# A decoder trunk on one core: the blocks of x's features spaced 136 words apart instead of 128, hi and lo parts shifted against each other

## Chip, cores, metric

One core of one Trainium2 chip runs the kernel. The metric is the device time of one execution in microseconds. Before the change three runs took 2485.54, 2493.08 and 2496.03 us; their median, 2493.08 us, is the time to compare with.

## What is computed

The input x is 256 tokens by 2048 features, float32. Two layers follow: a gated DeltaNet layer with its MLP, then a shared K/V projection, a differential-attention layer and its MLP. Nearly all of the arithmetic is in the products of 256 rows of activations with large weight matrices:

```
def gated_deltanet(x, w_in, conv_w, a_log, dt_bias, norm_w, w_out):
    p = x @ w_in                                 # 2048 -> 8192 + 32
    qkv = causal_conv_silu(p[..., :GDN_CONV_CH], conv_w)
    ...                                          # beta, g from the last 32 columns; delta rule
    return o.reshape(B, S, GDN_V_WIDTH) @ w_out  # 2048 -> 2048

def sq_relu_mlp(x, w_up, w_down):                # 2048 -> 8192 -> 2048
    return jnp.square(jax.nn.relu(x @ w_up)) @ w_down

def reference(x, ...):
    for l in range(DEPTH):                       # DEPTH = 2
        h = gated_deltanet(...) if l < N_A_LAYERS else diff_attention(..., k_sh, v_sh, ...)
        x = layer_norm(ALPHA * x + h, ln_g[l, 0], ln_b[l, 0])
        x = layer_norm(ALPHA * x + sq_relu_mlp(x, w_up[l], w_down[l]), ln_g[l, 1], ln_b[l, 1])
        if l == N_A_LAYERS - 1:
            k_sh, v_sh = shared_kv(x, shared_w_kv)   # 2048 -> 4096
    return x
```

## The kernel before

Every large product runs with the activations as the stationary operand of TensorE (loaded by LDWEIGHTS, 128 features by 128 tokens) and the weights streaming past as the moving operand, 512 columns at a time. To keep float32 accuracy both are split into a high and a low part of type float32r, and three matmuls, hi*hi, hi*lo and lo*hi, are accumulated (lines 174, 175, 176 in `product`). Each of the three has a LDWEIGHTS of its own.

`run` walks over the products: for each step of usually four k-tiles it takes token tile 0, then token tile 1; within a token tile the k-tiles in turn, within a k-tile the two column groups g of 512 columns. A k-tile thus gives six matmuls in a row, 174, 175, 176 for g = 0 and again for g = 1. Between the steps `pump` puts smaller pieces of work (convolution, scores, transposes) on TensorE.

The activations of a product come from one of two places:

- `xhl`, one constant tile, holds the features of the residual stream: for each part (hi, lo), token tile t and k-tile k a block of 128 tokens on 128 partitions. It is the stationary operand of x @ w_in, of both MLPs' w_up, of w_kv and of w_q: 30 products of 192 matmuls. `load_x` fills it first, `ln_apply` after each layer norm, both through `to_features` (four transposes by TensorE, then `split`: hi by ScalarE on line 78, lo by VectorE on line 79).
- blocks `blk` of 8 KB hold everything else: the squared ReLU for w_down, the outputs of both mixers for w_out and w_o. These are 20 products of 192 matmuls.

The moving operand is always a tile `wh` or `wl`, which `load_weights` makes from a DMA'd tile `wr` (ScalarE line 78, VectorE or GpSimd line 79). `gates` is the one place where x's features are the moving operand: on lines 424 and 425 the 32 columns of beta and alpha (in a `blk`) are stationary, and per k-tile one matmul streams hi and lo together (512 columns) and one streams hi alone (256 columns).

Where the tiles lie matters here. In the built program `xhl` begins at byte 17024 of each partition, which is 128 past a multiple of 512. Its blocks are 512 bytes apart, its token tiles 8 KB, its parts 16 KB, so that every block begins 128 past a multiple of 512. The pools `raw`, `hi`, `lo`, `blk` and `sm` follow the constants; the first `wh` begins at byte 69952, the first `wl` at 94528, the first `blk` at 119104, the first `sm` at 209216, each 320 past a multiple of 512, and all of their buffers and column groups are multiples of 512 further.

```
        self.sm_pool = pool("sm", 8)
        ...
        self.xhl = self.const.tile([P, 2, NT, KD, P], F32R, name="xhl")
    ...
    def x_stat(self, k, part, t):
        return self.xhl[:, part, t, k]
```

Of the kernel before, what the change touches and what calls it, by code (L numbers as in the profile page):

```python
# [27 lines left out]
SC = 4  # L28
ALPHA = 4.0**0.25
# [6 lines left out]
class Trunk:  # L36
    """Products run with the activations as the stationary operand and the weights streaming past them.

    Both operands are split exactly into two parts of 12 significant bits (float32r); three passes,
    hi*hi + hi*lo + lo*hi, give a float32 product. Activations for a product are kept with the features  # L40
    on the partitions, [128, (hi, lo), token tile, k-tile, token]; everything else is [token, feature].
    """

    def __init__(self, ctx, tc):
        self.tc, self.nc = tc, tc.nc
        pool = lambda name, bufs, **kw: ctx.enter_context(tc.tile_pool(name=name, bufs=bufs, **kw))
        nc = self.nc
        self.const = pool("const", 1)
        self.raw = pool("raw", 4)
        self.hi = pool("hi", 6)  # L50
        self.lo = pool("lo", 6)
        self.blk_pool = pool("blk", 11)
        self.sm_pool = pool("sm", 8)
        self.tiny = pool("tiny", 3)
        self.dram = pool("dram", 2, space=bass.MemoryType.DRAM)
        self.acc = pool("acc", 4, space=PSUM)
        self.ps_pool = pool("ps", 4, space=PSUM)
        self.plan, self.units, self.chain, self.pending, self.last = [], deque(), deque(), deque(), None
        self.ident = self.const.tile([P, P], F32, name="ident")
        make_identity(nc, self.ident)  # L60
        self.xhl = self.const.tile([P, 2, NT, KD, P], F32R, name="xhl")
        self.mask = self.const.tile([P, T], F32, name="mask")
        self.head_w = self.const.tile([P, P], F32, name="head_w")
# [17 lines left out]
    def rsqrt(self, dst, x, shape):  # L81
        """dst = x ** -0.5 for x > 0 (float32 accuracy: a guess from the exponent and three Newton steps)."""
        v = self.nc.vector
        y, t = self.small(shape, "rsq_y"), self.small(shape, "rsq_t")
        v.tensor_scalar(y.bitcast(I32), x.bitcast(I32), -0.5, float(0x5F3759DF), op0=ALU.mult, op1=ALU.add)
        for i in range(3):
            v.tensor_tensor(t, y, y, op=ALU.mult)
            v.scalar_tensor_tensor(t, t, -0.5, x, op0=ALU.mult, op1=ALU.mult)
            v.scalar_tensor_tensor(dst if i == 2 else y, t, 1.5, y, op0=ALU.add, op1=ALU.mult)

    def rsqrt_column(self, dst, x):
        """rsqrt of a column [128, 1] in fewer steps: (y y x - 3) y, Newton's step less its factor -1/2.

        The guess is scaled by a with -8192 a^27 = 1, which the three factors left out multiply back to 1.
        """
        v = self.nc.vector
        y, t = self.small([1], "rsq_y1"), self.small([1], "rsq_t1")
        a = -(8192.0 ** (-1.0 / 27.0))
        guess = RSQRT_GUESS - 2.0**31
        v.tensor_scalar(y.bitcast(I32), x.bitcast(I32), -0.5, guess, op0=ALU.mult, op1=ALU.add)  # L100
        for i, c in enumerate((3 * a**2, 12 * a**6, 768 * a**18)):
            v.scalar_tensor_tensor(t, y, x, y, op0=ALU.mult, op1=ALU.mult)
            last = v.scalar_tensor_tensor(dst if i == 2 else y, t, c, y, op0=ALU.subtract, op1=ALU.mult)
        return last

    def after(self, ins):
        """What is traced inside takes its turn on the engine of ins behind it."""
        return self.tc.issue_after(ins.ins) if ins is not None else nullcontext()

    def x_stat(self, k, part, t):  # L110
        return self.xhl[:, part, t, k]

    @staticmethod
    def act_stat(act):
        return lambda k, part, t: Trunk.act_view(act[k // 4])[:, part, t, k % 4]

    def gemm(self, nk, wsrc, stat, evac, pre=None, rate=1, need=None, cuts=None):
        """Plans a product: evac(g, t, psum) gets out[token tile t, columns g * 512 ..] of the 1024 columns of wsrc(k)."""
        self.plan.append((nk, wsrc, stat, evac, pre, rate, need, cuts or [SC] * (nk // SC)))

    def run(self):
# [4 lines left out]
        for j, (i, s, n) in enumerate(steps):  # L126
# [8 lines left out]
            for t in range(NT):  # L135
                # at the end of the second token tile one bank is done before the other, and evacuated meanwhile
# [41 lines left out]
    def later(self, fn, *args):  # L178
        """Work on the side of the products: emitted between them, a unit at a time."""
        self.units.append((fn, args))  # L180

    def soon(self, fn, *args):
        """A step of an evac that the tensor engine takes a few products later, when its operand is ready."""
        self.pending.append((fn, args))

    def pump(self, n):
        """Emits n units, and one of the slow chain, whose steps wait for transfers."""
# [12 lines left out]
    def transpose4(self, src):  # L200
        """[128, 512] -> PSUM [128, 4, 128], each 128 x 128 block transposed."""
# [5 lines left out]
    def to_features(self, src, dst, t):  # L207
        """src [128 tokens, 512] -> dst [128 features, (hi, lo), token tile, 4, 128 tokens] at token tile t."""
        self.split(dst[:, 0, t], dst[:, 1, t], self.transpose4(src))

    @staticmethod
    def act_view(a):
        return a.rearrange("p (s t k q) -> p s t k q", s=2, t=NT, k=4)
# [12 lines left out]
    def load_x(self, x):  # L226
        """The features of x by quarters: the first at once, the others between the first products."""
# [3 lines left out]
        def turn(t, q):  # L231
            with self.after(self.last):
                self.to_features(r[t][:, cut(q)], self.xhl[:, :, :, q * 4 : q * 4 + 4], t)
# [27 lines left out]
    def ln_apply(self, ln, t, q):  # L261
# [5 lines left out]
        if ln["out"] is None:  # L267
            self.to_features(xc, self.xhl[:, :, :, q * 4 : q * 4 + 4], t)
# [3 lines left out]
    def ln_finish(self, ln, t, own):  # L272
        """The last normalisation of a token tile: chunks below own on DVE, the others on ACT and Pool beside it."""
# [13 lines left out]
    def residual(self, n, alpha, ln=None):  # L287
        """The evac that adds a product's columns n * 1024 .. to the residual, and normalises it after the last."""
# [26 lines left out]
    def ends(n):  # L315
        """Before a normalisation the first token tile ends early, so that its rows are ready when the second ends."""
        return [5, 5, 6] if n == D // C - 1 else None

    def project_out(self, w, act, g, b, pre=None, need=None, out=None):
        """residual <- LayerNorm(alpha * residual + act @ w)."""  # L320
# [44 lines left out]
    def gated_deltanet(self, x, w_in, conv_w, a_log, dt_bias, norm_w, w_out, g, b, out=None):  # L365
        """The delta rule over all 256 tokens at once, two blocks of 128.

        With k2 = 2 k etc. (silu(y) = (tanh(y / 2) + 1) y / 2), S = |k2|^2 + 4 eps and c = beta / S:
        M = I + strict((k2 k2^T) c_j decay_ij), M y = v sqrt(S) / 2, o = 2 |q2|^-1 dk^-1/2 tril((q2 k2^T) c_j decay_ij) y.
        Matrices are kept transposed, [j, i]; the inverses of M's diagonal blocks are built from 32 x 32 ones.  # L370
        """
# [4 lines left out]
        mask = self.mask  # t <= i  # L376
        after = one.tile([P, P], F32R, name="g_after")  # t > j
# [31 lines left out]
        def gates():  # L409
            """beta = sigmoid(b), g = -exp(a_log) softplus(a + dt_bias) in two parts."""  # L410
# [6 lines left out]
            # the 32 columns four times over: float32r takes a stationary operand of 128  # L417
# [3 lines left out]
            for k in range(KD):  # L421
                xk = self.xhl[:, :, :, k]
                c = slice(k * P, (k + 1) * P)
                nc.tensor.matmul(pv4, wh[:, c], xk, start=(k == 0), stop=False, skip_group_check=True)
                nc.tensor.matmul(pv4[:, 0], wl[:, c], xk[:, 0], start=False, stop=(k == KD - 1), skip_group_check=True)
# [21 lines left out]
            # log(1 + e) = 2 atanh(e / (2 + e))  # L447
# [14 lines left out]
        def conv(raw, h, ct, dst):  # L462
            """Causal convolution and 2 silu of heads h, h + 1 of raw [channel, head, token] to dst [channel, 2, token]."""
# [48 lines left out]
        def score(hf, H, h):  # L512
            """U = (k k^T) c decay and A = (q k^T) c decay of heads h, h + 1, transposed."""
# [43 lines left out]
        def inv_gather(hf):  # L557
            """The 64 diagonal 32 x 32 blocks of the half, one to a partition."""
# [43 lines left out]
        def inv_merge(hf):  # L602
            """Y = the transposed inverses of the 16 128 x 128 blocks, from 32 to 64 to 128."""
# [28 lines left out]
        def solve(hf, gi, H):  # L632
            """Four heads: y, then o and its norm with the norm's weight (the gate follows with z)."""
# [124 lines left out]
    def diff_attention(self, w_kv, w_q, lam_params, subln_w, w_o, g, b, out=None):  # L758
# [27 lines left out]
        def heads(name, follow=None):  # L786
            """The evac that puts a product's heads with the features on the partitions: [128, head, token]."""
# [15 lines left out]
        def prob(hh, h, t, kb):  # L803
            """Where the transposed probabilities of a head's blocks lie: (0, 0), (1, 0), (1, 1)."""
# [3 lines left out]
        def score(kT, qT, hh, h, t):  # L808
            """Heads h, h + 1 of a half, query tile t; the two row tiles of a score go to banks of their own."""
# [40 lines left out]
        def values(hh, gi, t, v):  # L850
            """Four heads: probabilities @ v, the norm of each head, and the features for w_o."""
# [101 lines left out]
```

## Time and profile before

| What | Value |
|---|---|
| median of three runs | 2493.08 us (2485.54 to 2496.03) |
| span of the profiled execution | 2493.5 us |
| PE busy (matmuls) | 2448.1 us, 98% |
| PEld busy (weight loads) | 1985.4 us, 80% |
| DVE, ACT, POOL busy | 1498.4 us (60%), 1078.3 us (43%), 89.3 us (4%) |
| matmuls with a stationary block of `xhl` on lines 174 to 176 | 3 x 1920, 399 to 403 ns each by the profile |
| matmuls with a stationary block of `blk` there | 3 x 1280, 389 to 390 ns each |
| traffic | 438.84 MB, mean 176 GB/s |

Matmuls are pipelined: the next one starts while the last is still shown as busy, so that durations of some 0.39 us overlap, and the busy time of PE says little. What a matmul costs in a row of them is the time from its start to the start of the next, called its pitch here; it is read from the timeline, as the distance of two starts over the number of matmuls between them. For the profiled execution only the span is given, no separate device time; it lies 0.4 us above the median of the runs.

### The profile page before, as it was taken

The numbers are of one execution on the slowest core, as the hardware profiler recorded it, in microseconds if no ns is written. First come the engines' busy times: TensorE is split into PE (matmuls) and PEld (weight loads), VectorE is DVE, ScalarE is ACT, GpSimd is POOL, SyncE is SP. The second block draws the span as 40 slices with busy tenths as digits, with TensorE's granted clock in tenths as the row PEclk, the third lists the DMA queues.
The fourth block names the chain that finished last, engine by engine and source line by source line (L and its number), as shares of the span: only waits on it lengthen the run. The fifth ranks groups of instructions, "written<-read, shape, count | busy, mean of one in ns | idle before, by whom it ended". The sixth has DMA issues, their size and how long they took to land.

```text
span 2493.5 us, 30465 instructions
## 1 busy us (share of the span) xinstructions
PE 2448.1 (98%) x11492; PEld 1985.4 (80%) x11492; DVE 1498.4 (60%) x2333; ACT 1078.3 (43%) x1474; POOL 89.3 (4%) x94
## 2 busy tenths in 40 slices
PE   8999999999999999999998999999999999999997
PEld 6887888887888888888887877778788888888886
DVE  4789789567554554554557465665755554555556
ACT  4545445333443433434433464653443443443442
POOL 0010010002000000000002000000200000000001
PEclk9999999899999999999999999999999999999999
DMA  6545345464555556565554545454455555656553
GB/s 226 153 136 173 114 133 181 128 235 153 186 182 190 172 199 213 172 211 183 185 197 149 176 137 169 152 170 168 159 195 194 177 186 185 212 176 213 179 194 123
DMA packets 120212, 438.84 MB, mean 176 GB/s; under 512 B 13761, under 2 KB 13793, under 8 KB 119041
## 3 DMA queue, kind: packets, MB, share of 16 engines
q1 hardware_dynamic: 115920, 420.79, 51.2%
q0 software_dynamic: 2560, 11.13, 1.4%
q10 hardware_dynamic: 1584, 4.98, 0.5%
q8 instruction: 90, 1.47, 0.2%
q14 instruction: 58, 0.47, 0.1%
HBM read 433.70 MB, written 3.15 MB: 175 GB/s over the span
## 4 chain that ended last, share of the span: by engine, by line
PE 91%; DVE 5%; DMA 2%; issue 1%; ACT 1%; POOL 0%; SPq 0%; ACTq 0%; POOLq 0%; DVEq 0%
PE acc L175 28%; PE acc L176 28%; PE acc L174 27%; PE ps L204 3%; DVE wl L79 1%; DMA wr<-in_gdn_w_in_dram 1%; DVE blk L266 1%; DVE blk L265 1%; PE ps L818 1%; PE ps L549 1%; ACT wh L78 1%; PE ps L484 0%; DMA wr<-in_mlp_w_up_dram 0%; PE ps L620 0%; PE ps L616 0%
## 5 line engine op out<-in xcount | busy, mean ns | idle before, releaser
L79 DVE TENSOR_TENSOR wl<-wr,wh 128x1024 fp32r<-128x1024 f32 x785 | 954.9, 1227 | 694.3 <-ACT wh L78 671.2
L78 ACT CAST wh<-wr 128x1024 fp32r<-128x1024 f32 x800 | 831.8, 1052 | 969.4 <-PE acc L176 781.2
L174 PE MATMUL acc<-wh,xhl 128*128 128x512 f32 x1920 | 774.2, 403 | 0.1
L175 PE MATMUL acc<-wl,xhl 128*128 128x512 f32 x1920 | 768.5, 400 | 3.7 <-POOL wl L79 2.9
L176 PE MATMUL acc<-wh,xhl 128*128 128x512 f32 x1920 | 764.8, 399 | 0.0
L174 PE MATMUL acc<-wh,blk 128*128 128x512 f32 x1280 | 499.5, 390 | 0.0
L176 PE MATMUL acc<-wh,blk 128*128 128x512 f32 x1280 | 498.9, 390 | 0.0
L175 PE MATMUL acc<-wl,blk 128*128 128x512 f32 x1280 | 498.5, 389 | 0.0
L175 PEld LDWEIGHTS acc<-wl,xhl 128*128 128x128 f32 x1920 | 364.4, 190 | 86.4 <-POOL wl L79 4.2
L174 PEld LDWEIGHTS acc<-wh,xhl 128*128 128x128 f32 x1920 | 364.6, 190 | 84.9 <-issue 1.7
L176 PEld LDWEIGHTS acc<-wh,xhl 128*128 128x128 f32 x1920 | 363.5, 189 | 84.1
L176 PEld LDWEIGHTS acc<-wh,blk 128*128 128x128 f32 x1280 | 240.3, 188 | 50.0
L175 PEld LDWEIGHTS acc<-wl,blk 128*128 128x128 f32 x1280 | 240.4, 188 | 49.5
L174 PEld LDWEIGHTS acc<-wh,blk 128*128 128x128 f32 x1280 | 240.3, 188 | 49.6
L293 DVE SCALAR_TENSOR_TENSOR blk<-blk,acc 128x512 f32<-128x512 f32 x80 | 54.6, 684 | 85.2 <-PE acc L176 85.2
L204 PE MATMUL ps<-ident,sm 128*128 128x128 f32 x512 | 81.1, 274 | 1.4 <-DVE sm L868 1.2
L204 PEld LDWEIGHTS ps<-ident,sm 128*128 128x128 f32 x512 | 62.0, 141 | 24.8 <-PE acc L176 6.7
L78 ACT CAST blk<-ps 128x512 fp32r<-128x512 f32 x80 | 46.9, 586 | 71.3 <-PE ps L204 71.3
L347 DVE TENSOR_TENSOR sm<-sm 128x512 f32<-128x512 f32 x64 | 44.3, 693 | 54.7 <-ACT sm L346 54.3
L79 DVE TENSOR_TENSOR blk<-ps,blk 128x512 fp32r<-128x512 f32 x80 | 55.0, 688 | 30.8 <-ACT blk L78 30.8
L346 ACT ACTIVATE sm<-acc 128x512 f32<-128x512 f32 x64 | 38.3, 599 | 67.7 <-PE acc L176 64.5
L470 DVE SCALAR_TENSOR_TENSOR sm<-blk,g_cw,sm 128x255 f32<-128x255 f32 (+2 forms) x144 | 60.9, 476 | 0.0
(202 smaller groups left out, 1048.4 us busy)
## 6 DMA issues: line engine op xcount, KB each, us to landing
wr<-in_mlp_w_up_dram SPq DMA_DIRECT2D x256, 512.0 KB, 4.7
wr<-in_mlp_w_down_dram SPq DMA_DIRECT2D x256, 512.0 KB, 5.1
wr<-in_gdn_w_in_dram SPq DMA_DIRECT2D x128, 512.0 KB, 4.4
wr<-in_shared_w_kv_dram SPq DMA_DIRECT2D x64, 512.0 KB, 4.9
wr<-in_gdn_w_out_dram SPq DMA_DIRECT2D x32, 512.0 KB, 5.4
wr<-in_diff_w_q_dram SPq DMA_DIRECT2D x32, 512.0 KB, 4.6
wr<-in_diff_w_o_dram SPq DMA_DIRECT2D x32, 512.0 KB, 4.8
blk<-in_ln_g_dram POOLq DMA_DIRECT2D x4, 1024.0 KB, 7.2
```

The source lines that it names most:

```text
L78: self.nc.scalar.copy(hi, src)
L79: (engine or self.nc.vector).tensor_tensor(lo, src, hi.bitcast(F32), op=ALU.subtract)
L174: mm(ps, xh, wh[:, c], start=(k == 0), stop=False)
L175: mm(ps, xh, wl[:, c], start=False, stop=False)
L176: self.last = mm(ps, xl, wh[:, c], start=False, stop=(k == nk - 1))
L204: self.nc.tensor.transpose(pt[:, i], src[:, i * P : (i + 1) * P], self.ident)
L265: v.scalar_tensor_tensor(xc, xc, ln["mv", t][:, 0:1], ln["g"][:, c], op0=ALU.subtract, op1=ALU.mult)
L266: v.scalar_tensor_tensor(xc, xc, ln["rs", t], ln["b"][:, c], op0=ALU.mult, op1=ALU.add)
L293: self.nc.vector.scalar_tensor_tensor(rc, rc, alpha, ps, op0=ALU.mult, op1=ALU.add)
L346: self.nc.scalar.activation(a, ps, AF.Relu)
L347: self.nc.vector.tensor_tensor(a, a, a, op=ALU.mult)
L470: v_.scalar_tensor_tensor(y[:, i, d:], u[:, : T - d], w(j), y[:, i, d:], op0=ALU.mult, op1=ALU.add)
```

## The change

`xhl` becomes a tile of 2 rows of 2 x 16 x 136 + 4 words. A block is still 128 words, but the next begins 136 words (544 bytes) further, and the lo part begins 4 words into its row, which with the 4 words at the end of the hi row makes 32 bytes beyond a multiple of 512. `x_view` hands out the two parts as separate views, and everything that used `xhl` goes through it. In the built program `xhl` still begins at 17024; block (hi, t, k) now begins 128 + 32 k past a multiple of 512, block (lo, t, k) 160 + 32 k. Since `xhl` is 2080 bytes longer, all tiles behind it move: `wh` begins at 72032, `wl` at 96608, `blk` at 121184, each 352 past a multiple of 512. The pool `sm` has seven buffers instead of eight. In `gates` hi and lo no longer lie at one stride, so the matmul of 512 columns is cut in two of 256.

```
+XP = P + 8
...
-        self.sm_pool = pool("sm", 8)
+        self.sm_pool = pool("sm", 7)
...
-        self.xhl = self.const.tile([P, 2, NT, KD, P], F32R, name="xhl")
+        self.xhl = self.const.tile([P, 2, NT * KD * XP + 4], F32R, name="xhl")
...
+    def x_view(self, k0, k1):
+        parts = [self.xhl[:, s, s * 4 : s * 4 + NT * KD * XP] for s in range(2)]
+        return [a.rearrange("p (t k q) -> p t k q", t=NT, k=KD)[:, :, k0:k1, :P] for a in parts]
+
     def x_stat(self, k, part, t):
-        return self.xhl[:, part, t, k]
+        return self.x_view(k, k + 1)[part][:, t, 0]
...
     def to_features(self, src, dst, t):
-        self.split(dst[:, 0, t], dst[:, 1, t], self.transpose4(src))
+        self.split(dst[0][:, t], dst[1][:, t], self.transpose4(src))
...
         if ln["out"] is None:
-            self.to_features(xc, self.xhl[:, :, :, q * 4 : q * 4 + 4], t)
+            self.to_features(xc, self.x_view(q * 4, q * 4 + 4), t)
...
             for k in range(KD):
-                xk = self.xhl[:, :, :, k]
+                xh, xl = (v[:, :, 0] for v in self.x_view(k, k + 1))
                 c = slice(k * P, (k + 1) * P)
-                nc.tensor.matmul(pv4, wh[:, c], xk, start=(k == 0), stop=False, skip_group_check=True)
-                nc.tensor.matmul(pv4[:, 0], wl[:, c], xk[:, 0], start=False, stop=(k == KD - 1), skip_group_check=True)
+                nc.tensor.matmul(pv4[:, 0], wh[:, c], xh, start=(k == 0), stop=False, skip_group_check=True)
+                nc.tensor.matmul(pv4[:, 1], wh[:, c], xl, start=False, stop=False, skip_group_check=True)
+                nc.tensor.matmul(pv4[:, 0], wl[:, c], xh, start=False, stop=(k == KD - 1), skip_group_check=True)
```

The view of `blk` (`act_view`) returns its two parts as a list too, with the same addresses inside the block; `load_x` and `act_stat` are rewritten to match. The order of the instructions stays as it was on every engine but TensorE, and there it differs only in `gates`. On TensorE, at the first k-tile of `gates`, the order before is this (line 424 is the matmul of 512 columns; `acc` and `ps` are PSUM tiles, the number behind a name counts the tiles):

```order
L176 MATMUL acc_647<-wh_689,xhl_89 128x512
L424 MATMUL ps_570<-xhl_89,blk_565 128x512
L174 MATMUL acc_731<-wh_671,xhl_89 128x512
L175 MATMUL acc_731<-wl_672,xhl_89 128x512
L176 MATMUL acc_731<-wh_671,xhl_89 128x512
```

and with the change:

```order
L183 MATMUL acc_663<-wh_705,xhl_89 128x512
L432 MATMUL ps_570<-xhl_89,blk_565 128x256
L433 MATMUL ps_570<-xhl_89,blk_565 128x256
L181 MATMUL acc_747<-wh_687,xhl_89 128x512
L182 MATMUL acc_747<-wl_688,xhl_89 128x512
L183 MATMUL acc_747<-wh_687,xhl_89 128x512
```

Two matmuls of 256 columns stand where one of 512 stood; the products around them (lines 174 to 176, now 181 to 183) are in the same places.

## Rows read from the trace of the kernel before

**Rows 1.** The page: the span, the busy time of PE, and the chain of work that ended last (shares of the span, by engine and then by engine, tile and line).

```profile
span 2493.5 us, 30465 instructions
PE 2448.1 (98%) x11492; PEld 1985.4 (80%) x11492; DVE 1498.4 (60%) x2333; ACT 1078.3 (43%) x1474; POOL 89.3 (4%) x94
...
PE 91%; DVE 5%; DMA 2%; issue 1%; ACT 1%; POOL 0%; SPq 0%; ACTq 0%; POOLq 0%; DVEq 0%
PE acc L175 28%; PE acc L176 28%; PE acc L174 27%; PE ps L204 3%; DVE wl L79 1%; DMA wr<-in_gdn_w_in_dram 1%; DVE blk L266 1%; DVE blk L265 1%; PE ps L818 1%; PE ps L549 1%; ACT wh L78 1%; PE ps L484 0%; DMA wr<-in_mlp_w_up_dram 0%; PE ps L620 0%; PE ps L616 0%
```

**Rows 2.** The groups of instructions by line, the products' matmuls and two of their weight loads (out<-moving,stationary; count | busy us, mean ns of one | idle us before them).

```profile
L174 PE MATMUL acc<-wh,xhl 128*128 128x512 f32 x1920 | 774.2, 403 | 0.1
L175 PE MATMUL acc<-wl,xhl 128*128 128x512 f32 x1920 | 768.5, 400 | 3.7 <-POOL wl L79 2.9 <-DVE wl L79 0.8
L176 PE MATMUL acc<-wh,xhl 128*128 128x512 f32 x1920 | 764.8, 399 | 0.0
L174 PE MATMUL acc<-wh,blk 128*128 128x512 f32 x1280 | 499.5, 390 | 0.0
L176 PE MATMUL acc<-wh,blk 128*128 128x512 f32 x1280 | 498.9, 390 | 0.0
L175 PE MATMUL acc<-wl,blk 128*128 128x512 f32 x1280 | 498.5, 389 | 0.0
L176 PEld LDWEIGHTS acc<-wh,xhl 128*128 128x128 f32 x1920 | 363.5, 189 | 84.1
L176 PEld LDWEIGHTS acc<-wh,blk 128*128 128x128 f32 x1280 | 240.3, 188 | 50.0
```

**Rows 3.** The timeline of PE at the first and the last of 174 matmuls in an unbroken row with stationary blocks of `xhl`, in the last layer's w_up (start us, us, instruction).

```profile
2299.22 0.40 PE L174 MATMUL acc<-wh,xhl 128*128 128x512 f32 x1
2299.46 0.39 PE L175 MATMUL acc<-wl,xhl 128*128 128x512 f32 x1
...
2339.36 0.40 PE L175 MATMUL acc<-wl,xhl 128*128 128x512 f32 x1
2339.59 0.40 PE L176 MATMUL acc<-wh,xhl 128*128 128x512 f32 x1
```

**Rows 4.** The timeline of PE at the first and the last of 371 matmuls in an unbroken row with stationary blocks of `blk`, in the last layer's w_down.

```profile
2395.47 0.39 PE L175 MATMUL acc<-wl,blk 128*128 128x512 f32 x1
2395.70 0.40 PE L176 MATMUL acc<-wh,blk 128*128 128x512 f32 x1
...
2479.14 0.39 PE L175 MATMUL acc<-wl,blk 128*128 128x512 f32 x1
2479.36 0.39 PE L176 MATMUL acc<-wh,blk 128*128 128x512 f32 x1
```

**Rows 5.** The busy time of each engine in these two stretches (stretch and its length; busy us and count of PE, PEld, DVE, ACT, POOL; granted clock; DMA share, GB/s).

```profile
2299.30:2339.50 40.20, 40.20 (x174) 32.40 (x173) 20.05 (x19) 15.83 (x17) 0.00 (x0) 1.00 0.63 209
2395.50:2479.30 83.80, 83.80 (x371) 69.39 (x370) 46.43 (x55) 29.16 (x29) 2.01 (x2) 1.00 0.47 158
```

**Rows 6.** The timeline of PE at the end of `gates`, where `xhl` is the moving and a `blk` the stationary operand.

```profile
88.09 0.28 PE L425 MATMUL ps<-xhl,blk 128*128 128x256 f32 x1
88.21 0.40 PE L424 MATMUL ps<-xhl,blk 128*128 128x512 f32 x1
88.44 0.28 PE L425 MATMUL ps<-xhl,blk 128*128 128x256 f32 x1
88.56 0.40 PE L424 MATMUL ps<-xhl,blk 128*128 128x512 f32 x1
```

**Rows 7.** The groups by line again, ScalarE and VectorE: writes of four blocks of 128 in a row (`xhl`) and of four blocks of 128 with gaps between them (lines 498 and 797).

```profile
L78 ACT CAST xhl<-ps 128x512 fp32r<-128x512 f32 x32 | 18.5, 587 | 39.1 <-PE ps L204 38.5
L498 ACT COPY blk<-ps 128x512 f32<-128x512 f32 x24 | 13.7, 589 | 7.0 <-PE ps L204 7.0
L79 DVE TENSOR_TENSOR xhl<-ps,xhl 128x512 fp32r<-128x512 f32 x32 | 21.3, 685 | 4.2 <-ACT xhl L78 3.9
L797 DVE COPY blk<-ps 128x512 f32<-128x512 f32 x16 | 10.8, 688 | 19.2 <-PE ps L204 19.2
```

**Rows 8.** The timeline of POOL and of ACT: a DMA into an `sm` tile in `gates` and the instruction that reads it.

```profile
58.10 1.21 POOL L413 DMA_DIRECT2D sm<-in_gdn_w_in_dram  x1 [54.39 <-PE ps L204]
...
76.33 1.90 ACT L78 CAST blk<-sm 128x2048 fp32r<-128x2048 f32 x1
```

**Rows 9.** The page's DMA queue of the weights (packets, MB, share of 16 engines), and the waits: who waited for what, us in total, times, longest us.

```profile
q1 hardware_dynamic: 115920, 420.79, 51.2%
...
ACT wh L78 <- PE acc L176: 781.2, 496, 11.4
...
PE acc L175 <- POOL wl L79: 2.9, 3, 1.7
...
PE acc L175 <- DVE wl L79: 0.8, 1, 0.8
```

**Rows 10.** The groups by line, VectorE: line 470 (in `conv`) works on 255, 254 or 253 words of an `sm` tile that begin 4, 8 or 12 bytes past the tile's own start; line 843 is the same kind of operation on 256 words from the start on.

```profile
L470 DVE SCALAR_TENSOR_TENSOR sm<-blk,g_cw,sm 128x254 f32<-128x254 f32 x48 | 21.5, 476 | 0.0
L470 DVE SCALAR_TENSOR_TENSOR sm<-blk,g_cw,sm 128x253 f32<-128x253 f32 x48 | 21.5, 475 | 0.0
L470 DVE SCALAR_TENSOR_TENSOR sm<-blk,g_cw,sm 128x255 f32<-128x255 f32 x48 | 21.5, 476 | 0.0
L843 DVE SCALAR_TENSOR_TENSOR sm<-sm,z 128x256 f32<-128x256 f32 x16 | 7.0, 479 | 0.0
```

More of the change, by code (lines that the diff above doesn't have):

```diff
@@ L108, in after @@
         return self.tc.issue_after(ins.ins) if ins is not None else nullcontext()
+    def x_view(self, k0, k1):
+        parts = [self.xhl[:, s, s * 4 : s * 4 + NT * KD * XP] for s in range(2)]
+        return [a.rearrange("p (t k q) -> p t k q", t=NT, k=KD)[:, :, k0:k1, :P] for a in parts]
     def x_stat(self, k, part, t):
-        return self.xhl[:, part, t, k]
+        return self.x_view(k, k + 1)[part][:, t, 0]
     @staticmethod
     def act_stat(act):
-        return lambda k, part, t: Trunk.act_view(act[k // 4])[:, part, t, k % 4]
+        return lambda k, part, t: Trunk.act_view(act[k // 4])[part][:, t, k % 4]
     def gemm(self, nk, wsrc, stat, evac, pre=None, rate=1, need=None, cuts=None):
@@ L207, in to_features @@
     def to_features(self, src, dst, t):
-        self.split(dst[:, 0, t], dst[:, 1, t], self.transpose4(src))
+        self.split(dst[0][:, t], dst[1][:, t], self.transpose4(src))
     @staticmethod
     def act_view(a):
-        return a.rearrange("p (s t k q) -> p s t k q", s=2, t=NT, k=4)
+        v = a.rearrange("p (s t k q) -> p s t k q", s=2, t=NT, k=4)
+        return [v[:, 0], v[:, 1]]
     @staticmethod
@@ L232, in turn @@
             with self.after(self.last):
-                self.to_features(r[t][:, cut(q)], self.xhl[:, :, :, q * 4 : q * 4 + 4], t)
+                self.to_features(r[t][:, cut(q)], self.x_view(q * 4, q * 4 + 4), t)
         for c in (cut(0), slice(G, D)):
```

## Prediction

> **What bounds the kernel now.** Read the page first: PE is busy for 98% of the span, and the chain that ended last runs over PE for 91% of it, 83% in the three matmuls of `product` alone [rows 1]. So the time is the sum of what TensorE does, and a nanosecond on each product matmul is 9.6 us on the whole (5760 with a block of `xhl`, 3840 with a `blk`) [rows 2]. The groups by line come second, because they show the difference on which everything here turns: the same operation, with the same moving tiles `wh` and `wl` and the same shapes, is shown with 399 to 403 ns where the stationary block lies in `xhl`, and with 389 to 390 ns where it lies in a `blk` [rows 2]. Third comes the timeline, since the durations overlap and only distances between starts count. In an unbroken row with `xhl` the 173 steps from 2299.22 to 2339.59 us take 40.37 us, 233.35 ns each [rows 3]. In an unbroken row with `blk` the 370 steps from 2395.47 to 2479.36 us take 83.89 us, 226.73 ns each [rows 4]. The two differ by 6.62 ns, or 38.1 us over the 5760 matmuls. The view by stretches rules out the usual reasons: the clock is 1.00 in both, and PE is busy throughout [rows 5]. A late weight tile is no reason either, since PE waited only 2.9 and 0.8 us for a `wl` in the whole span [rows 9]; and the LDWEIGHTS, 188 to 189 ns, are shorter than either pitch [rows 2].
>
> What differs, then, is where the stationary block lies. The weights begin 320 bytes past a multiple of 512; a `blk` does too, so the distance between stationary and moving operand is 0 (counted in 512s), while a block of `xhl` (128 past) stands 192 off. `gates` shows the same with the roles exchanged: there `xhl` streams past a `blk`, and the matmul of 512 columns takes 88.44 - 88.21 = 0.23 us to the next start, the slow pitch, not the fast one, as far as two decimals tell [rows 6]. So it looks as if the pair decides, not the stationary operand alone. But these are only two points: distance 0 is fast, distance 192 in either sense is slow, and no row shows another.
>
> **The change, term by term.** *The 5760 product matmuls on `xhl`.* With the change the moving tiles begin 352 past a multiple of 512, a hi block at 128 + 32 k and a lo block at 160 + 32 k. The distances are 32 (k - 7) and 32 (k - 6): each of 16 steps of 32 bytes is taken by one k-tile in sixteen, for hi and for lo. One of the 16 is distance 0, two are 192 off in one sense or the other, and 13 are unseen. The bounds are the two known pitches: at 226.73 ns everywhere the term is -38.1 us, at 233.35 ns it is 0. Beyond them nothing is excluded on either side, since a new distance may be better than 0 or worse than 192. I take the middle, 230.04 ns, as the mean of two samples of a function of which the change takes all sixteen: -3.31 ns x 5760 = **-19.1 us**. Another reason for the middle is that the distance now changes at every k-tile, after six matmuls, so that none of the long even rows of before can settle.
>
> *The 3840 product matmuls on `blk`.* Weights and blocks move by the same 32 bytes and stay at distance 0: 0 us. What it costs if the absolute start matters is a rival below.
>
> *`gates`.* One pair takes 88.44 - 88.09 = 0.35 us now, its 256 columns 88.21 - 88.09 = 0.12 us [rows 6]. With the change there are three matmuls of 256 columns, 0.36 us. Sixteen times 0.01 us is **+0.2 us**, and with the rounding of the rows between -0.1 and +0.4. All of it is on TensorE, and so on the path. The 24 products with other constants as stationary operand in the scores stay where they were, relative to the moving tile, since the constants behind `xhl` move by the same 32 bytes as everything else.
>
> *The writes into `xhl`.* `split` now writes four blocks with gaps instead of one run: 32 times by ScalarE (587 ns now) and by VectorE (685 ns). The nearest rows, copies of 512 words into four separate blocks, take 589 and 688 ns [rows 7]. At +2 and +3 ns each, 32 of each are under 0.2 us, mostly beside products: 0.
>
> *Seven `sm` buffers.* The order of the instructions is unchanged, so only waits for a free buffer can grow. The tightest place is the Pool queue, where the DMA of line 413 already waited for the transpose that freed its tile. It is issued at 58.10 us and read by ScalarE at 76.33 us [rows 8]. With seven buffers it waits for a transpose one or two later, which follow each other within a k-step of 24 products, 24 x 0.2333 = 5.6 us. That is well inside the 18 us. Behind it on Pool there are only the two small loads of line 439 and 440: 0. If the cover were gone, the price would be at most those 5.6 us, once.
>
> *Weight tiles at other addresses.* `wr`, `wh`, `wl` now begin on an odd multiple of 32 bytes. For VectorE a start 4, 8 or 12 bytes off costs nothing visible: 475 to 476 ns beside 479 ns for the aligned operation [rows 10]. The DMA queue of the weights uses 51.2% of its engines, and ScalarE waits 781.2 us for TensorE to free a `wh`, so some per cent on the loads are hidden [rows 9]: 0.
>
> The sum is -19.1 + 0.2 = -18.9 us. The profiled execution had a span of 2493.5 us, 0.4 us over the median of the runs, and no other time is given for it; 2493.5 - 18.9 - 0.4 gives **2474.2 us**, 0.8% less than the median.
>
> **The rivals.** *All distances but a few are as good as 0.* Then every block of `xhl` runs at 226.7 ns: 2493.1 - 38.1 + 0.2 = 2455.2 us. For it: the slow pitch might be a clash at one particular distance. Against it: two of two other-than-zero readings (192 either way) are slow.
>
> *Nothing happens.* The slow pitch may belong to the distance in general, with 0 the one good value, or to the place of `xhl` low in the memory, whatever its fine address. Then 1 of 16 blocks gains at best, 38.1 / 16 = 2.4 us: 2491 to 2493.3 us. For it: the 174 matmuls of rows 3 pass over many blocks at one and the same pace, and `gates`, which uses the same tile, is as slow [rows 3, 6]. Against it: nothing but the lack of a reason why low addresses should be slow. The Trainium skill goes further in this direction: "TensorE: Matmul & The Clock Gate" (section "Step-by-step: what each phase is for") says that the streaming operand and LDWEIGHTS have independent read ports in SBUF, so that loading the next weights takes nothing from the running matmul; by it no address of a stationary block could matter, and the change would give 0. The trace does not bear the rule out as it stands, since rows 3 and 4 differ by 6.6 ns with the same moving tiles.
>
> *Slower: streams that start off a multiple of 64 bytes.* Before, every stationary and moving operand of the products began at a multiple of 64; with the change all weights, all `blk` and half of the blocks of `xhl` begin 32 past one. If TensorE reads in wider pieces than 32 bytes, each stream has one piece more. No row shows a start like that on TensorE. Priced at the one step that the rows show, 6.6 ns, it costs 2880 x 6.6 ns = 19 us if only x's odd blocks pay (it then cancels the gain, or gives 2512 us without one), and 9600 x 6.6 ns = 63 us if all moving streams pay, 2556 us. It decides from 18.9 us / 9600 = 2.0 ns per matmul on (no gain left), and from 3.3 ns on the kernel is slower by over 0.5%. For it: no row shows such a start. Against it: VectorE does not mind [rows 10]. The Trainium skill speaks against it too: "SBUF — State Buffer" (section "Specifications (TRN2)") gives lines of 16 bytes, in which every start here, before and after, is still the start of a line; no run here shows it for TensorE.
>
> **How the numbers follow.** The middle case, pitches on `xhl` from about 228.3 to 231.1 ns, has a chance of 0.38; all as good as distance 0 or better 0.14; nothing happens 0.28; slower 0.20, of which a good half is the dear form or a part of it beyond 2515 us. The 0.5% that a measurement of this kernel can tell are 12.5 us, or 2.2 ns per matmul on `xhl`. The first two cases are faster by more than that, so faster 0.52, same 0.28, slower 0.20. The range goes from 2446 us, some 9 us beyond the all-good case, since no row bounds the pitch from below, to 2515 us, just beyond the cheap form of the slower one. That leaves out about 0.18: some 0.12 above, and below the pitches under 225 ns.
>
> **What the changed profile would show.** In an unbroken row of the last w_up the distance of starts should be near 230 ns, and differ from k-tile to k-tile: near 226.7 where the distance is 0 (k = 7 for hi, k = 6 for lo), near 233 at 192 off. In w_down it should stay at 226.7 ns. The gates' matmuls should follow each other by 0.12 us. The prediction is wrong in its main step if the pitch on `xhl` stays at 233 for all k-tiles, and wrong in what it takes for free if the pitch on `blk` moves at all, or if PE starts to wait for a `wl` or an `sm`.

## The result and the profile after

The changed kernel takes 2481.72 us (median of five runs, 2476.10 to 2483.91) beside 2493.88 us before: a ratio of 0.9947, with a 95% interval of 0.9925 to 0.9969, 12.2 us less. Run again later, the ratio was 0.9977 (0.9958 to 0.9995). What mostly sets the two apart is the mean granted clock of an execution, which varies from 0.985 to 0.996 in the runs here, and the time goes with it, about 2.1 us for 0.001 (the kernel before took 2480.7 and 2483.3 us at 0.996, 2503.7 and 2504.0 us at 0.986). The changed kernel's first five runs had 0.992 to 0.996; for the runs before beside them no clock is on record. Executions of equal clock agree much better: at 0.994 the kernel before took 2485.3 to 2487.7 us (seven runs, median 2486.3) and the changed one 2479.4 to 2480.9 us (four runs, median 2479.7). So the change is worth about **6.6 us**, 0.27%, which is less than the first comparison says; a difference of one step of 0.001 in the clock would move this by 2 us, but the runs at 0.989 and at 0.993 give some 6 us too. Below, times are compared at equal clock where runs allow it, and pitches are taken from stretches with the clock at 1.00, the higher of its two levels.

The page, and the products' groups by line (line | busy us, mean ns of one | idle before), which answer to [rows 1, 2]:

```profile
span 2481.9 us, 30498 instructions
PE 2438.5 (98%) x11508; PEld 1984.7 (80%) x11508; DVE 1498.1 (60%) x2333; ACT 1077.9 (43%) x1474; POOL 89.0 (4%) x94
```
```profile
L181 PE MATMUL acc<-wh,xhl 128*128 128x512 f32 x1920 | 770.4, 401 | 0.1
L182 PE MATMUL acc<-wl,xhl 128*128 128x512 f32 x1920 | 766.7, 399 | 3.4 <-POOL wl L81 2.7 <-DVE wl L81 0.7
L183 PE MATMUL acc<-wh,xhl 128*128 128x512 f32 x1920 | 761.3, 397 | 0.0
L181 PE MATMUL acc<-wh,blk 128*128 128x512 f32 x1280 | 500.0, 391 | 0.0
L81 DVE TENSOR_TENSOR xhl<-ps,xhl 128x512 fp32r<-128x512 f32 x32 | 21.3, 684 | 4.5 <-ACT xhl L80 4.1
L80 ACT CAST xhl<-ps 128x512 fp32r<-128x512 f32 x32 | 18.5, 587 | 39.2 <-PE ps L211 38.7
```

The matmuls on `xhl` became 1 to 2 ns shorter, those on `blk` did not, and the writes into `xhl` stayed at 587 and 684 ns in spite of the gaps. The timeline of PE over the same two stretches as in [rows 3, 4], 174 matmuls in the last w_up and 371 in the last w_down, and the clock there:

```profile
2288.17 0.39 PE L181 MATMUL acc<-wh,xhl 128*128 128x512 f32 x1
...
2328.30 0.39 PE L183 MATMUL acc<-wh,xhl 128*128 128x512 f32 x1
...
2383.89 0.40 PE L182 MATMUL acc<-wl,blk 128*128 128x512 f32 x1
...
2467.81 0.39 PE L183 MATMUL acc<-wh,blk 128*128 128x512 f32 x1
```
```profile
2288.20:2328.20 40.00, 40.00 (x174) 32.41 (x173) 20.07 (x19) 15.86 (x17) 0.00 (x0) 1.00 0.64 209
2384.00:2467.70 83.70, 83.70 (x371) 69.32 (x370) 46.35 (x55) 29.08 (x29) 1.98 (x2) 1.00 0.47 157
```

On `xhl` 173 steps take 40.13 us, 231.97 ns each, where it was 233.35. On `blk` 370 steps take 83.92 us, 226.8 ns, as before. Over all matmuls on `xhl` that are followed by the next within 245 ns (some 5300 of the 5760; the others stand before a transpose or other work, or in a stretch of lower clock), the mean pitch fell from 233.33 to 232.09 ns: 1.24 ns x 5300 = 6.6 us, as much as the gain. The agreement is no closer than some 2 us, as no_spacing and d256 below show.

### The profile page after: what moved, and what is told of

It reads as the page before. It is cut to its first block, busy times and chain, and to the rows that moved or that the text cites. A ratio compares the mean times of both kernels' runs of the same rounds, so it can differ in the third digit from the quotient of the medians.

```text
span 2481.9 us, 30498 instructions
## 1 busy us (share of the span) xinstructions
PE 2438.5 (98%) x11508; PEld 1984.7 (80%) x11508; DVE 1498.1 (60%) x2333; ACT 1077.9 (43%) x1474; POOL 89.0 (4%) x94
## 4 chain that ended last, share of the span: by engine, by line
PE 90%; DVE 6%; DMA 2%; issue 1%; ACT 1%; POOL 0%; SPq 0%; ACTq 0%; POOLq 0%; DVEq 0%
PE acc L182 27%; PE acc L181 27%; PE acc L183 27%; PE ps L211 3%; DVE wl L81 1%; DMA wr<-in_gdn_w_in_dram 1%; DVE blk L274 1%; DVE blk L273 1%; PE ps L827 1%; PE ps L558 1%; PE ps L493 0%; DMA wr<-in_mlp_w_up_dram 0%; DVE blk L595 0%; PE ps L629 0%; ACT wh L80 0%
```

## Experiments

Two theories were tested first. **Pair theory**: the pitch depends on the distance between the stationary block and the weights that stream. **Place theory**: `xhl` is slow because of where it lies, and what hurt was the spacing of 512 bytes. With constant distance a row of products has time to settle, so the first runs give each distance a long row.

**map32.** The kernel before, its eight groups of four k-tiles (token tile x quarter) 32 bytes further apart each, seven `sm` buffers.

```
+XG = 4 * P + 8
+XO = 0
...
-        self.xhl = self.const.tile([P, 2, NT, KD, P], F32R, name="xhl")
+        self.xhl = self.const.tile([P, 2, NT * 4 * XG + 64], F32R, name="xhl")
...
+    def x_group(self, q):
...
+        a = self.xhl[:, :, XO : XO + NT * 4 * XG].rearrange("p s (t g r) -> p s t g r", t=NT, g=4)
+        return a[:, :, :, q, : 4 * P].rearrange("p s t (k q) -> p s t k q", k=4)
```

Expected: 

> The kernel before, with the eight groups of four k-tiles (two token tiles, four groups) spaced 32 bytes further apart each and seven sm buffers: a row of 24 or more matmuls at one distance between stationary block and weights, eight distances in one run (320, 352, 384, 416, 448, 480, 0, 32, counted in 512s). Pair theory (the settled pitch depends on the distance alone): 226.7 ns at distance 0, 233.3 ns at 320, values between 224 and 236 at the others, steady within a row. Place theory (xhl is slow because of where it lies, and the blocks' spacing of 512 bytes is what hurt): blocks inside a group are 512 bytes apart again, so 233.3 ns at all eight. Settling theory (the change lost part of its gain because the distance changes at each k-tile): the mean of the eight settled pitches is lower than the 231.2 ns of the changed kernel by more than 1 ns. Time 2455 to 2495 us.

**map16.** The same with all of `xhl` 4 words further in its tile (`XO = 4`).

Expected: 

> As map32, with all of xhl 16 bytes further: distances 336, 368, 400, 432, 464, 496, 16, 48. Pair theory: values between those of the neighbours 32 bytes apart; if starts inside a piece of 32 bytes cost something by themselves, all eight are above those of map32 by 3 ns or more. Place theory: 233.3 ns at all. Time 2455 to 2520 us.

**map8.** The same with groups 8 bytes apart (`XG = 4 * P + 2`, 38 words further), around distance 0.

Expected: 

> As map32, with the eight groups spaced 8 bytes: distances 472, 480, 488, 496, 504, 0, 8, 16 (counted in 512s). Pair theory: a dip around distance 0 with 226.7 ns from 496 to 0 or 8, 228 to 229 ns at 16, 233.4 ns at 480, and perhaps a pitch below 226.7 ns somewhere inside the dip. A theory in which only whole pieces of 16 or 32 bytes count: steps, the same pitch for all distances inside a piece. Place theory, already in doubt: 233 ns at all.

Measured, from the distances of starts, matmuls from the seventh of an unbroken row on (83 to 444 of them for each distance), in one run of each (2488, 2488 and 2482 us). Distances are counted in 256s here, since d256 below shows that 256 does what 0 does. The distance of the kernel before, 192 below the weights, is 320 in 512s and 64 in this table:

```
map32   0: 227.0   32: 233.3   64: 233.4   96: 234.2   128: 232.4   160: 233.5   192: 229.8   224: 233.4
map16  16: 228.6   48: 233.4   80: 232.0  112: 233.3   144: 229.0   176: 230.2   208: 231.9   240: 227.0
map8  216: 229.3  224: 233.2  232: 231.1  240: 227.2   248: 233.3     0: 226.9     8: 230.8    16: 233.4
```

So the distance does set the pitch, by up to 7 ns. 226.7 ns is the floor, nearly reached at 0 and 240 (226.9 to 227.2) and nowhere undercut, and 233.3 ns is not one bad value but a common one: of the eight distances that the change takes, those of map32, five lie at 233.3 to 234.2. Their mean is 232.1, which refutes the settling theory: steady rows at these distances would be no faster than the change is. (The 231.2 ns that the expectation names for the changed kernel is about its step from the first to the second of the three matmuls; its mean is 232.1.)

Steps of 8 bytes count too, and not as a smooth dip: map8 has 233.3 at 248 between 227.2 at 240 and 226.9 at 0, and map16 has 80 and 144 faster than both neighbours, against what was expected. The timeline of PE in map32 shows one group settle (distances in 512s): 384 ends, 0 begins at 2320.36, 416 begins at 2325.84.

```profile
2320.12 0.40 PE L183 MATMUL acc<-wh,xhl 128*128 128x512 f32 x1
2320.36 0.40 PE L181 MATMUL acc<-wh,xhl 128*128 128x512 f32 x1
...
2321.75 0.39 PE L181 MATMUL acc<-wh,xhl 128*128 128x512 f32 x1
...
2325.60 0.40 PE L183 MATMUL acc<-wh,xhl 128*128 128x512 f32 x1
2325.84 0.39 PE L181 MATMUL acc<-wh,xhl 128*128 128x512 f32 x1
...
2331.21 0.39 PE L183 MATMUL acc<-wh,xhl 128*128 128x512 f32 x1
```

The first six steps at distance 0 take 1.39 us, 232 ns each, the next 17 take 3.85 us, 226.5 ns each. The 23 steps at 416 behind them take 5.37 us, 233.5 ns each. In this group the fast pitch shows after six matmuls; over all groups of map32 at distance 0 the mean of a step inside the group is within 1 ns of 226.7 from the ninth on. The changed kernel never keeps a distance that long: its hi and lo blocks stand 32 bytes apart, and a k-tile takes hi, hi, lo, hi, hi, lo, so that a distance holds for three matmuls in a row at most.

One entry does not fit a pitch by distance alone: 16 gave 228.6 in map16, where single steps jump between 227 and 232 to 234, and 233.4 in map8, there in the last group of a product, whose matmuls stand in another order. At some distances, it seems, more than one rhythm can hold.

**map32b.** map32 with 8 words left free behind `xhl`, so that all weights and all `blk` begin 32 bytes past a multiple of 64.

Expected: 

> As map32, with 32 more bytes left free behind xhl, so that all weights and blk begin 32 bytes past a multiple of 64 (352 in 512s) and the eight groups stand at distances 288, 320, 352, 384, 416, 448, 480, 0. Pair theory: each distance has the pitch that map32 gave it, within 1 ns: 227 at 0, 233.4 at 320, 234.2 at 352, 232.4 at 384, 233.5 at 416, 229.8 at 448, 233.4 at 480, and the unseen 288 like 32, 233.3. Theory of absolute starts: the pitch goes with the group instead, so the group that stood at 0 keeps 227 and now stands at 480.

Measured: 0: 227.1, 288: 233.3, 320: 233.4, 352: 234.2, 384: 232.2, 416: 233.3, 448: 229.0, 480: 233.4, `blk` 226.7 ns (one run, 2497.13 us at a clock of 0.987). The pitch goes with the distance, within 0.8 ns, and not with the group, as the pair theory expected. Absolute starts off a multiple of 64 cost nothing.

**d0** and **d256.** The kernel before with 80 or 16 words left free behind `xhl`, which puts every block at a constant distance 0 or 256.

```
         self.xhl = self.const.tile([P, 2, NT, KD, P], F32R, name="xhl")
+        self.const.tile([P, 16], F32, name="pad1")
```

Expected of d0: 

> The kernel before, with 320 bytes left free behind xhl: every block of xhl stands at distance 0, as the blocks of blk do. Pair theory: 226.7 ns on xhl, 38 us less, 2455 us, ratio 0.985. Place theory: 233.3 ns, 2493 us, ratio 1.000.

Expected of d256: 

> The kernel before, with 64 bytes left free behind xhl, nothing else: every weight tile and blk moves by 64 bytes, every block of xhl stands at distance 256 instead of 320. Pair theory with a period of 256 bytes: 226.7 ns on xhl, 38 us less, 2455 us, ratio 0.985. Pair theory with a period of 512: unknown, 226 to 236 ns, 2450 to 2510 us. Place theory: 233.3 ns, 2493 us, ratio 1.000.

Measured: d0 2461.95 us, ratio 0.9900 (0.9869 to 0.9931); d256 2464.15 us, ratio 0.9908 (0.9877 to 0.9939). The place theory is refuted, and distance 256 does what 0 does: the mean pitch on `xhl` over all rows is 227.6 ns in both. In the changed kernel, too, which takes each distance and the one 256 away, the two agree within about 1 ns. The time fell less than the 38 us expected. The groups by line and the timeline of PE of d256, the last w_up (174 matmuls):

```profile
L175 PE MATMUL acc<-wh,xhl 128*128 128x512 f32 x1920 | 764.0, 398 | 0.4 <-ACT wh L79 0.3
L175 PE MATMUL acc<-wh,blk 128*128 128x512 f32 x1280 | 499.4, 390 | 0.0
```
```profile
2270.49 0.39 PE L175 MATMUL acc<-wh,xhl 128*128 128x512 f32 x1
...
2309.71 0.39 PE L177 MATMUL acc<-wh,xhl 128*128 128x512 f32 x1
```

39.22 us / 173 = 226.7 ns, the pitch of `blk`. The mean over all rows is 227.6 ns, since each interruption costs some slow steps: 5.7 ns x some 5280 = 30 us less. At a clock of 0.994 the three runs of d256 and d256_again take 2460.7, 2462.0 and 2463.4 us, 23 to 26 us under the median of before. Some 5 us of the 30 are not found in the time; 2.4 us of them are seen, in a wait of PE for the DMA of the inverses that grew from 0.5 to 2.9 us. The rest is open.

**blk64.** The kernel before with 64 bytes left free in front of the pool `blk`.

```
+        pool("gap", 1).tile([P, 16], F32, name="gap")
         self.blk_pool = pool("blk", 11)
```

Expected: 

> The kernel before with 64 bytes left free in front of the pool of blk: the blocks of w_down, w_out and w_o stand at distance 64 to the weights instead of 0, xhl stays at 320. Pair theory: 233.3 ns on the 3840 matmuls with a blk instead of 226.7, 25 us slower, 2510 to 2525 us. Place theory: 226.7 ns on blk, no change.

Measured: 2517.05 us at a clock of 0.992 (one run; before 2492.26 at that clock). The timeline of PE over the 371 matmuls of the last w_down:

```profile
2415.16 0.39 PE L176 MATMUL acc<-wl,blk 128*128 128x512 f32 x1
...
2501.49 0.40 PE L177 MATMUL acc<-wh,blk 128*128 128x512 f32 x1
```

86.33 us / 370 = 233.3 ns, against 226.73 in [rows 4]: 64 bytes of empty memory slow every w_down, w_out and w_o, by 6.6 ns x 3840 = 25 us. The pair decides, for `blk` as for `xhl`.

The rest takes the change apart.

**no_spacing.** The changed kernel with `XP = P`, no shift of lo, and 520 words left free behind `xhl` so that everything else stays in place.

Expected: 

> The changed kernel with the spacing alone undone: blocks 128 words apart and no shift of lo, but the tiles behind xhl where the change puts them, seven sm buffers and gates in three matmuls. All blocks of xhl stand at the constant distance 288. Pair theory: 233.3 ns as at distance 32, so 2487 to 2494 us, ratio to before 1.000 (0.998 to 1.002). If the gain of the change lay in its other parts (sm, gates, the moved tiles): 2476 us, ratio 0.995.

Measured: ratio 0.9988 (0.9968 to 1.0007); pitch 233.2 ns. The timeline of PE, the last w_up (174 matmuls, 233.3 ns each):

```profile
2295.00 0.39 PE L182 MATMUL acc<-wh,xhl 128*128 128x512 f32 x1
...
2335.36 0.39 PE L184 MATMUL acc<-wh,xhl 128*128 128x512 f32 x1
```

At a clock of 0.995 it takes 2481.9 to 2482.0 us, before 2484.5 to 2486.0. The pitch explains 0.9 us of these 3; some 2 us may belong to the other parts of the change (the moved tiles, `sm`, `gates`) or to the runs. They do not carry the gain, but up to a third of it may be theirs.

**no_lo_shift.** The changed kernel with hi and lo blocks of a k-tile at the same distance.

```
-        self.xhl = self.const.tile([P, 2, NT * KD * XP + 4], F32R, name="xhl")
+        self.xhl = self.const.tile([P, 2, NT * KD * XP], F32R, name="xhl")
+        self.const.tile([P, 8], F32, name="pad")
...
-        parts = [self.xhl[:, s, s * 4 : s * 4 + NT * KD * XP] for s in range(2)]
+        parts = [self.xhl[:, s, 0 : NT * KD * XP] for s in range(2)]
```

Expected: 

> The changed kernel with the shift of the lo part undone and the tiles behind xhl held in place: hi and lo blocks of a k-tile at the same distance, sixteen distances over the k-tiles. Pair theory: each k-tile near the pitch of its distance, mean 230.5 to 232 ns, 2478 to 2486 us, ratio 0.994 to 0.998, as the change itself. If the change needs hi and lo apart from each other: 233 ns and ratio 1.000.

Measured: ratio 0.9987 (0.9964 to 1.0009); pitch 232.54 ns, 0.8 ns less than before, not the 1.24 ns of the change. At equal clock the spacing alone is worth more than the ratio says: at 0.995 two runs took 2480.2 and 2480.9 us, 4 to 6 us under before. The timeline of PE, the last w_up (174 matmuls, 232.7 ns each):

```profile
2306.53 0.39 PE L182 MATMUL acc<-wh,xhl 128*128 128x512 f32 x1
...
2346.78 0.40 PE L184 MATMUL acc<-wh,xhl 128*128 128x512 f32 x1
```

The mean pitches by the distance of a matmul's own block, first over the steps to a matmul at the same distance (2555 of 5296 in the changed kernel, 4307 of 5251 in no_lo_shift), then over all steps:

```
distance (in 256s)      0      32     64     96     128    160    192    224
same next, changed      230.1  230.9  233.7  230.6  230.0  232.3  230.0  233.6
same next, no_lo_shift  230.5  233.1  233.7  233.1  233.0  233.8  230.9  233.3
all steps, changed      232.4  232.0  232.8  231.0  231.8  232.9  231.5  232.5
all steps, no_lo_shift  230.9  232.6  233.3  232.7  232.8  233.7  231.0  233.2
```

With hi and lo 32 bytes apart, 32, 96 and 128 lose 2 to 3 ns on the steps between equal distances. The steps at which the distance changes are slower: in the changed kernel they take 232.8 ns on average, the others 231.4. Over all steps the shift of lo makes 0 and 192 slower and the rest faster. So the pitch depends on the sequence of distances, not only on each one.

**lo_only.** The changed kernel with `XP = P` and 512 words left free behind `xhl`: blocks 128 words apart, lo still 32 bytes off.

Expected: 

> The changed kernel with blocks 128 words apart but the lo part still 32 bytes off the hi part; the tiles behind xhl stay in place. Hi blocks at distance 288, lo blocks at 320, the same for all k-tiles. Sum theory (each matmul has the settled pitch of its own distance): 233.3 ns, for both distances have it. Sequence theory (the pitch depends on how the distance changes from one matmul to the next, and a change between hi and lo breaks the slow rhythm): 230 to 232 ns, most of the gain of the change without the spacing.

Measured: 2480.28 us at a clock of 0.993 (one run; before 2488.1 to 2489.0, the changed kernel 2481.7 to 2483.9 at the same clock). The timeline of PE, the last w_up:

```profile
2285.00 0.39 PE L182 MATMUL acc<-wh,xhl 128*128 128x512 f32 x1
...
2324.99 0.39 PE L184 MATMUL acc<-wh,xhl 128*128 128x512 f32 x1
```

39.99 us / 173 = 231.2 ns, although both distances, 288 and 320, settle at 233.3 ns when constant. By step, over all rows, hi to hi takes 230.0 ns, hi to lo 233.0, lo to hi 231.0. At this one pair of distances the shift of lo gives the whole gain of the change and more: its mean over all rows is 231.4 ns, the changed kernel's 232.1. The spacing of 136 words, which gives 0.8 ns by itself, adds nothing beside it. Other pairs of distances were not tried.

**after_again** and **d256_again**, on one chip.

Expected of after_again: 

> The changed kernel once more, beside the kernel with 64 bytes free behind xhl. Every theory left: ratio to before 0.995 (0.993 to 0.997), mean pitch on xhl 231 to 232 ns, as at first.

Expected of d256_again: 

> The kernel before with 64 bytes left free behind xhl, once more, on the same chip as the changed kernel. Pair theory: 227.6 ns on xhl within rows, ratio to before 0.989 (0.986 to 0.992), 12 to 20 us faster than the changed kernel. If the first result was the chip's: ratio as the changed kernel's, 0.995.

Measured: 0.9977 (0.9958 to 0.9995), and 0.9908 (0.9883 to 0.9933) at 2464.04 us. The changed kernel's ratio missed the 0.993 to 0.997 expected of it, which took the first comparison at its word; the pitches came again as at first, 232.1 and 227.6 ns. The kernel before with 64 empty bytes beats both kernels, before and changed, the latter by 22 us in the medians of that chip (2486.16 and 2464.04 us) and by about 18 us at equal clock.

## Why the prediction was right, and where not

*What bounds the kernel* was right: the pitch of the 5760 matmuls on `xhl` carries the gain, and nothing else moved by more than some 2 us.

*That the pair decides, not the stationary block alone,* was right: blk64 slowed `blk` by the same 6.6 ns, and in map32b, where the weights and `blk` moved together, `blk` kept its 226.7 ns and the pitches on `xhl` followed the distance. One reading behind it was no evidence, though: the 0.23 us of `gates` in [rows 6] cannot tell the two pitches apart, since 0.2267 and 0.2333 us both round to it. And in d256, with its operands at distance 256, that step takes 232 to 240 ns as well, so `gates` does not show the distance at all. So "distance 192 in either sense is slow" had one reading behind it, not two; 192 in the other sense, the 192 of the table of map32, settles at 229.0 to 229.8 ns.

*The term of -19.1 us* had the right sign and was mis-sized: it measured -6.6 us. The step that failed is "the mean of two samples of a function of which the change takes all sixteen". Of the two known points, one was the bottom of a narrow dip and the other a common value. The eight settled values of map32 have a mean of 232.1 ns, not 230.04. A third of the forecast gain was left because most of the distances that the change takes are nearly as slow as that of before. The pitches of two layouts cannot stand for a function with dips 8 to 16 bytes wide.

*That "the distance now changes at every k-tile, after six matmuls, so that none of the long even rows of before can settle"* was right in its conclusion and understates the change: it also changes between hi and lo, as map32 above says. So the pitches by k-tile did not come as forecast. Over all steps with a block at distance 0 the changed kernel runs at 232.4 ns, not at the 226.7 expected for k = 7 and k = 6, and at 96 at 231.0, 3 ns below the settled 234.2; by distance its means lie between 231.0 and 232.9, where the settled ones go from 227.0 to 234.2. That its mean over all is 232.1 too is, as far as the runs show, a coincidence. lo_only shows that a distance that changes between hi and lo is by itself enough for a gain, from 233.3 to 231.2 ns, and no_lo_shift that the spacing alone is worth 0.8 ns; how the two combine in the change stays open.

*What was put at nothing* held. `gates` issues its three matmuls in 0.36 us a k-tile, as said:

```profile
88.19 0.28 PE L434 MATMUL ps<-xhl,blk 128*128 128x256 f32 x1
88.31 0.28 PE L432 MATMUL ps<-xhl,blk 128*128 128x256 f32 x1
88.43 0.28 PE L433 MATMUL ps<-xhl,blk 128*128 128x256 f32 x1
88.55 0.28 PE L434 MATMUL ps<-xhl,blk 128*128 128x256 f32 x1
```

The loads into `sm` were issued 0.9 and 3.3 us later, and the first is still read 17 us after its issue (timelines of POOL and ACT, beside [rows 8]):

```profile
59.02 1.21 POOL L421 DMA_DIRECT2D sm<-in_gdn_w_in_dram  x1 [55.32 <-PE ps L211]
65.08 0.55 POOL L448 DMA_DIRECT2D sm<-in_gdn_a_log_dram  x1 [4.84 <-ACT wh L80]
...
76.10 1.90 ACT L80 CAST blk<-sm 128x2048 fp32r<-128x2048 f32 x1
```

*The rivals.* "All distances but a few are as good as 0" is refuted: it is the other way round. "Nothing happens" for the distance in general came near: 233.3 ns or a little more is the value of most of these distances, and at equal clock the gain of 0.27% is below what was called measurable; but the place of `xhl` in memory has no part in it. "Streams that start off a multiple of 64 bytes" cost nothing: `blk` kept 226.8 ns in the changed kernel, with all its operands at such starts, and map32b agrees. As to how the two operands meet: 64 empty bytes change the pitch of 3840 matmuls by 6.6 ns (blk64). The Trainium skill ("TensorE: Matmul & The Clock Gate", section "Step-by-step: what each phase is for") has a load of weights take nothing from the running matmul, since the two read ports are independent; the trace does not bear that out as it stands. Whether it is the load that slows the stream, and whether they meet in the memory or further on, no run here shows.

The forecast time, 2474.2 us, was 7.5 us under the measured median; by the gain at equal clock, 18.9 us stood against 6.6. That the median came even so near was luck in part: of the 12.2 us of the first comparison 5.6 do not stand at equal clock. And the range, 69 us wide, would also have held a kernel that did not change at all.

## What to carry to other kernels

When one operation shows two durations with the same shapes, compare the addresses of its operands modulo a few hundred bytes before anything else: here a pad of 64 bytes, one line, was worth 24 us and needed no new layout. Spreading addresses evenly takes the good distances with the bad, and the order in which they come counts as well; where one distance is known to be good from the same trace, put everything there. And a prediction for an unknown function should weigh that the known good point may be the exception.

## What the runs showed of the hardware

The start-to-start time of float32r matmuls of 512 columns, at a granted clock of 1.00, depends on the distance in memory between the block that LDWEIGHTS reads and the columns that stream, with a period of 256 bytes (0 and 256: 227.6 ns over all rows, both), from 226.7 ns (at 0) to 234.2 ns (96), in steps as fine as 8 bytes (240: 227.2, 248: 233.3, 0: 226.9, 8: 230.8). A row that comes to distance 0 from a slow one needs six to nine matmuls to reach the fast pitch, and a distance that changes between hi and lo blocks gives another pitch, 231.2 ns for 288 and 320, than either distance alone, 233.3 ns. Why these distances, and why the order matters, stays open.
